# The second feed-forward sweep of a hybrid decoder layer: low parts on VectorE, sums of the last weights in other sweeps

## The chip, the cores and the metric

The kernel runs on one core of a Trainium2 chip. The metric is the device time of one execution in microseconds; the median of three executions is given, and one further execution was profiled. Engines are named as in the profile: PE (TensorE, matmuls), DVE (VectorE), ACT (ScalarE), POOL or Pool (GpSimd), SP (SyncE, which here only issues transfers).

## What is computed

One layer: a modulated norm, a projection into gated DeltaNet heads and sliding-window attention heads, an output projection with a gated residual, then a second modulated norm and a gated feed-forward part with its residual. The change lies in the feed-forward part; before it come the last products of the output projection, whose tiles the text names `w_o`. With 1024 tokens, 1024 features and an inner width of 2816:

```python
mixed = jnp.concatenate([o_g, o_s], axis=-1) @ w_out[l]
x = x + gate1 * mixed

h2 = rms_norm(x, norm2_w[l]) * (1.0 + scale2) + shift2
ffn = (jax.nn.silu(h2 @ w_gate[l]) * (h2 @ w_up[l])) @ w_down[l]
x = x + gate2 * ffn
```

## The kernel before

All products are made to nearly full precision from a high and a low part of each operand: `split` (lines 192 and 193) rounds an operand on ACT to its high part and subtracts that from the operand on DVE or Pool for the low part. `mm_block` (lines 1360 to 1364) runs three matmuls for each pair of tiles: high by high, high by low, low by high. So the low part of the weights is wanted first by the third matmul.

The feed-forward products are made by a scheme of seven products of half-sized blocks in place of eight, which needs sums and differences of blocks. There are three stages.

- **First sweep**, eleven steps p = 0 to 10, one for each 256 columns of the inner width. `weights1` loads and splits two sets of tiles (w0, w1; high on ACT, low on Pool); 48 matmuls write the banks `ps_c`. ACT copies a first result out (`X`, line 1402, stored to XD), and the product of line 1408 makes `av`, stored to AD. In the first steps the rest of the second norm and the splits of its results (B, T) run on DVE, ACT and Pool, too.
- **Second sweep**, again p = 0 to 10. `weights2` loads, for each of the two matrices j (gate and up), `wa` and `wb` with two blocks each, makes four sums of 128x512 on DVE (lines 1429 to 1432), and splits five left sides (S2, S3, S1, A22, S4) for each j, high on ACT, low on Pool. Ten units of twelve matmuls write the banks `ps_S`; after each one DVE adds the bank to an earlier result (line 1466). A22 goes on in the bank of S3, S4 in that of S1. The results are made into six tiles of `ops`, stored to AD (line 1479); `ops` and `sg` have one buffer. The tiles of `weights2` come from a pool `px`, the split ones from `wg2`, with ten buffers of 128x1024.
- **Last products** P1, P2, P6, P7, P4, P5, P3: 924 matmuls into `ps_P`. Their left sides are blocks of the weights `wdown`, or sums of them that `down_sums` has stored in SD before (used from P6 on); their right sides are the slices of AD. `left` loads and splits the former (Pool makes the low parts), `slices` the latter (DVE does).

`down_sums` is a piece of work that belongs to no stage: 24 times it loads four blocks of `wdown` (tile `sd`, 512 KB, half of that in the last of each six), makes four sums on DVE and stores them. Fifteen calls stand in the first sweep's code and nine in the second's.

The order of PE's instructions is that of the code. For the other engines and for SP's queue a scheduler decides it within the limits that the code sets with `issue_after` and `high_priority`; each engine then works strictly in that order, and so does SP: a transfer whose buffer isn't free holds up all that stand behind it.

## Time and profile before

| | us |
|---|---|
| median of three executions | 1318.24 (1317.91 to 1318.87) |
| profiled execution, its own time | 1316.84 |
| span of the profiled execution | 1315.1 |
| first sweep, in the trace | about 654 to 779 |
| second sweep | 779.4 to 1099.6 |
| last products | from 1099.6 on |
| PE busy, whole span | 1193.2 |
| DVE busy, whole span | 904.9 |
| Pool busy, whole span | 626.5 |
| ACT busy, whole span | 537.3 |

The page gives busy time for each engine; matmuls are pipelined, so the distance from one start to the next tells the rate, not the length of one. A view of stretches gives busy time, the clock that TensorE was granted (1.00 is 2.4 GHz, 0.50 is 1.2 GHz) and the transfer rate. A view of waits adds up the idle time of an engine by what ended it. A timeline lists instructions in order, with the idle time ahead of each. Buffer numbers are left out of names in the trace: `wS` stands for wS20, wS31 and so on.

### The profile page before, as it was taken

How to read it: one execution, taken by the hardware profiler on the slowest of the kernel's cores; microseconds unless marked ns; L12 is line 12 of the kernel's file. 1: busy time of each engine (PE TensorE's matmuls, PEld its weight loads, DVE VectorE, ACT ScalarE, POOL GpSimd, SP SyncE). 2: the span in 40 equal slices, each digit the busy share in tenths (PEclk: the TensorE clock that was granted, in tenths of full speed). 3: DMA queues.
4: the chain of work that ended last, by engine and by line, in shares of the span. 5: the costliest groups of instructions: out<-in, count | busy, mean ns of one | idle time of the engine just before them, and what ended most of it. 6: DMA issues, size and time to landing. Idle time of an engine off the chain costs nothing.

```text
span 1315.1 us, 18978 instructions
## 1 busy us (share of the span) xinstructions
PE 1193.2 (91%) x6710; PEld 975.4 (74%) x6710; DVE 904.9 (69%) x1690; ACT 537.3 (41%) x1028; POOL 626.5 (48%) x453
## 2 busy tenths in 40 slices
PE   6868697896899799998889999999999999999998
PEld 5757576685788577777678888777777778888887
DVE  7999889979724667586864656777767786656430
ACT  4373555422433767533435542222322233544430
POOL 4667354534335334345435556454454454455440
PEclk7898899898999889999899999999999999999999
DMA  8637458485639845448685645555555467876651
GB/s 324 227 93 262 154 121 233 127 226 197 197 109 211 145 82 131 157 159 289 233 275 205 207 136 169 176 192 192 192 202 189 178 230 266 264 267 198 201 168 40
DMA packets 167214, 250.62 MB, mean 191 GB/s; under 512 B 40656, under 2 KB 106448, under 8 KB 165584
## 3 DMA queue, kind: packets, MB, share of 16 engines
q1 hardware_dynamic: 157520, 241.03, 56.5%
q0 software_dynamic: 9600, 8.39, 3.9%
q8 instruction: 53, 0.87, 0.3%
q14 instruction: 41, 0.34, 0.1%
HBM read 182.89 MB, written 66.45 MB: 190 GB/s over the span
## 4 chain that ended last, share of the span: by engine, by line
PE 39%; DVE 18%; DMA 11%; issue 4%; POOL 3%; ACT 2%; SPq 0%; DVEq 0%; ACTq 0%; POOLq 0%
PE ps_P L1363 5%; PE ps_P L1362 5%; PE ps_P L1364 5%; DMA wb<-in_wgate_dram 3%; DMA SD<-sd 3%; DMA sd<-in_wdown_dram 2%; PE ps_c L1362 2%; PE ps_c L1364 2%; PE ps_c L1363 2%; POOL wS L193 2%; DMA qb<-QS 2%; DVE wa L1432 1%; DVE xu L1466 1%; PE ps_gz L212 1%; DVE soltmp L817 1%
## 5 line engine op out<-in xcount | busy, mean ns | idle before, releaser
L193 POOL TENSOR_TENSOR wP<-rP,wP 128x512 fp32r<-128x512 f32 (+1 forms) x84 | 109.1, 1314 | 104.6 <-ACT wP L192 95.9
L1363 PE MATMUL ps_P<-t,wP 128*128 128x512 f32 x308 | 120.4, 391 | 0.0
L1362 PE MATMUL ps_P<-t,wP 128*128 128x512 f32 x308 | 120.4, 391 | 0.0
L1364 PE MATMUL ps_P<-t,wP 128*128 128x512 f32 x308 | 120.2, 390 | 0.0
L193 POOL TENSOR_TENSOR wS<-wa,wS 128x512 fp32r<-128x512 f32 x44 | 62.2, 1422 | 118.4 <-ACT wS L192 59.4
L1364 PE MATMUL ps_S<-T,wS 128*128 128x512 f32 x264 | 102.9, 390 | 0.3 <-POOL wS L193 0.3
L1363 PE MATMUL ps_S<-T,wS 128*128 128x512 f32 x264 | 102.9, 390 | 0.0
L1362 PE MATMUL ps_S<-T,wS 128*128 128x512 f32 x264 | 102.8, 389 | 0.0
L1429 DVE TENSOR_TENSOR ws<-wb 128x512 f32<-128x512 f32 x22 | 24.6, 1118 | 72.8 <-DMA wb<-in_wgate_dram 68.0
L192 ACT ACTIVATE wP<-rP 128x512 fp32r<-128x512 f32 (+1 forms) x84 | 47.3, 587 | 66.8 <-PE ps_P L1364 41.2
L1470 ACT ACTIVATE sg<-sg 128x512 f32<-128x512 f32 x33 | 20.9, 632 | 131.3 <-DVE sg L1466 131.2
L1362 PE MATMUL ps_c<-B,w 128*128 128x512 f32 x176 | 68.8, 391 | 1.3 <-ACT X L1402 1.3
L1364 PE MATMUL ps_c<-B,w 128*128 128x512 f32 x176 | 68.5, 389 | 0.0
L1363 PE MATMUL ps_c<-B,w 128*128 128x512 f32 x176 | 68.5, 389 | 0.0
L1362 PEld LDWEIGHTS ps_P<-t,wP 128*128 128x128 f32 x308 | 57.9, 188 | 12.6
L1364 PEld LDWEIGHTS ps_P<-t,wP 128*128 128x128 f32 x308 | 57.9, 188 | 12.5
L1363 PEld LDWEIGHTS ps_P<-t,wP 128*128 128x128 f32 x308 | 57.8, 188 | 12.4
L192 ACT ACTIVATE wS<-wa 128x512 fp32r<-128x512 f32 x44 | 26.6, 625 | 93.9 <-DVE wa L1431 68.3
L1364 PEld LDWEIGHTS ps_S<-T,wS 128*128 128x128 f32 x264 | 49.6, 188 | 11.1 <-POOL wS L193 0.7
L1362 PEld LDWEIGHTS ps_S<-T,wS 128*128 128x128 f32 x264 | 49.6, 188 | 10.5
L1363 PEld LDWEIGHTS ps_S<-T,wS 128*128 128x128 f32 x264 | 49.6, 188 | 10.4
L212 PE MATMUL ps_o<-mix,w_o 128*128 128x512 f32 x128 | 52.9, 413 | 4.1 <-ACT w_o L192 4.1
(507 smaller groups left out, 3575.5 us busy)
## 6 DMA issues: line engine op xcount, KB each, us to landing
ada<-in_ada_dram SPq DMA_DIRECT2D x48, 512.0 KB, 4.6
AD<-ops SPq DMA_DIRECT2D x11, 1536.0 KB, 5.2
rP<-SD SPq DMA_DIRECT2D x16, 704.0 KB, 5.4
sd<-in_wdown_dram SPq DMA_DIRECT2D x20, 512.0 KB, 5.7
SD<-sd SPq DMA_DIRECT2D x20, 512.0 KB, 3.5
rP<-in_wdown_dram SPq DMA_DIRECT2D x12, 704.0 KB, 5.9
XD<-X SPq DMA_DIRECT2D x22, 256.0 KB, 3.8
xu<-XD SPq DMA_DIRECT2D x22, 256.0 KB, 4.2
```

Of the source, the lines that this page charges most:

```text
L192: act.activation(out=r(hi), in_=src, func=AF.Copy)
L193: last = eng.tensor_tensor(out=r(lo), in0=src, in1=hi, op=ALU.subtract)
L212: pe.matmul(out, lhsT=r(lhs[0]), rhs=r(rhs[0]), start=first, stop=False)
L817: dve.tensor_tensor(out=tv[g], in0=bc(L[:, i, i + 1:32].unsqueeze(1), (P, i, 31 - i)), in1=bc(L[:, 0:i, i:i + 1], (P, i, 31 - i)), op=ALU. ...
L1362: pe.matmul(ps, lhsT=r(wh), rhs=r(xh), start=first and i == 0, stop=False, **kw)
L1363: pe.matmul(ps, lhsT=r(wh), rhs=r(xl), start=False, stop=False, **kw)
L1364: pe.matmul(ps, lhsT=r(wl), rhs=r(xh), start=False, stop=i == n - 1, **kw)
L1429: dve.tensor_tensor(out=s1, in0=a21, in1=a22, op=ALU.add)
L1432: dve.tensor_tensor(out=a12, in0=a12, in1=a11, op=ALU.subtract)
L1466: done["U"] = dve.tensor_tensor(out=out, in0=ps, in1=other, op=ALU.add)
L1470: act.activation(out=out, in_=out, func=AF.Silu)
```

## The change

`weights2` makes one tile for both matrices where there were two: five tiles of 128x1024 (a11, a12, a21, a22 and a sum) for each p, loaded by eight transfers of 256 KB in place of four of 512 KB. So there are four sums of 128x1024 instead of eight of 128x512, and five high parts on ACT and five low parts of 128x1024, these now on DVE instead of ten of 128x512 on Pool. The units run in the order S2, S3, S1, A22, S4, each for j = 0 and then j = 1. The additions that empty the banks get high priority.

`down_sums` takes two marks: its load is issued after one of them, its first sum after the other. In the first sweep it stands behind the store of X and behind av, with a list that tells how many calls belong to each p (again fifteen). In the second sweep there is one call in every other p, five in all; the last four follow the first four products of P1 in the code, with tiles of another pool.

```diff
@@ -24,7 +24,7 @@
 HD = 64
 NB = T // P
 FF = 2816
-FF_CHUNKS = (6, 6, 6, 4)
+SUMS1 = (1, 2, 1, 1, 1, 1, 1, 1, 2, 2, 2)
 ADA_TAGS = "bcd" * 5 + "bcde" * 4 + "d"
 ADA_ITER = 14
 ADA_DVE = ()
...
@@ -1375,13 +1376,17 @@
             split(w[:, 0, js], w[:, 1, js], raw[:, js], pool)
         return w
 
-    def down_sums(d, k0, k1):
-
-        t = rpre.tile([P, NP, P], F32, tag="r", name=f"sd{d}_{k0}")[:, 0:8].rearrange("p (a k) n -> p a k n", a=4)
+    def down_sums(d, k0, k1, load_after, sums_after, t=None):
+
+        if t is None:
+            t = rpre.tile([P, NP, P], F32, tag="r", name=f"sd{d}_{k0}")[:, 0:8]
+        t = t.rearrange("p (a k) n -> p a k n", a=4)
         n = k1 - k0
-        sp.dma_start(out=t[:, :, 0:n], in_=wdown[d][:, :, k0:k1])
+        with tc.issue_after(load_after.ins):
+            sp.dma_start(out=t[:, :, 0:n], in_=wdown[d][:, :, k0:k1])
         a11, a12, a21, a22 = (t[:, i, 0:n] for i in range(4))
-        dve.tensor_tensor(out=a22, in0=a21, in1=a22, op=ALU.add)
+        with tc.issue_after(sums_after.ins):
+            dve.tensor_tensor(out=a22, in0=a21, in1=a22, op=ALU.add)
         dve.tensor_tensor(out=a21, in0=a11, in1=a21, op=ALU.subtract)
         dve.tensor_tensor(out=a11, in0=a22, in1=a11, op=ALU.subtract)
         dve.tensor_tensor(out=a12, in0=a12, in1=a11, op=ALU.subtract)
@@ -1399,19 +1404,18 @@
                 mm_block(ps[j], lambda i: (w[a][:, 0, 4 * j + i], w[a][:, 1, 4 * j + i]), lambda i: B1[4 * a + i], 4, a == 0)
                 if a == 0:
                     x = t2(f"X{j}_{p}")
-                    done["X"] = act.activation(out=x, in_=ps[j], func=AF.Copy)
-                    sp.dma_start(out=XD[p, j], in_=x)
+                    act.activation(out=x, in_=ps[j], func=AF.Copy)
+                    done["X"] = sp.dma_start(out=XD[p, j], in_=x)
                 if (p, a, j) in ((0, 0, 1), (1, 0, 1)):
                     next(n2, None)
         av = t2(f"av{p}")
         act.activation(out=av, in_=ps[0], func=AF.Silu)
-        dve.tensor_tensor(out=av, in0=ps[1], in1=av, op=ALU.mult)
+        done["av"] = dve.tensor_tensor(out=av, in0=ps[1], in1=av, op=ALU.mult)
         sp.dma_start(out=AD[:, p, 0], in_=av)
-        with tc.issue_after(done["X"].ins):
-            for _ in range(2 if p in (0, 1, 2, 10) else 1):
-                down_sums(*sums.pop(0))
-            if 2 <= p < 10:
-                next(second)
+        if 2 <= p < 10:
+            next(second)
+        for _ in range(SUMS1[p]):
+            down_sums(*sums.pop(0), done["X"], done["av"])
 
 
     close_pools(2)
@@ -1420,25 +1424,24 @@
 
     def weights2(p):
 
-        src, out = {}, {}
-        for j in range(2):
-            wa, wb, ws = (px.tile([P, 2, 4, P], F32, tag="s4", name=f"w{x}{j}_{p}") for x in "abs")
-            sp.dma_start(out=wa.rearrange("p a k n -> p (a k) n"), in_=SRC[j][2 * p])
-            sp.dma_start(out=wb.rearrange("p a k n -> p (a k) n"), in_=SRC[j][2 * p + 1])
-            a11, a12, a21, a22, s1 = wa[:, 0], wa[:, 1], wb[:, 0], wb[:, 1], ws[:, 0]
-            dve.tensor_tensor(out=s1, in0=a21, in1=a22, op=ALU.add)
-            dve.tensor_tensor(out=a21, in0=a11, in1=a21, op=ALU.subtract)
-            dve.tensor_tensor(out=a11, in0=s1, in1=a11, op=ALU.subtract)
-            dve.tensor_tensor(out=a12, in0=a12, in1=a11, op=ALU.subtract)
-            src[j] = {"S2": a11, "S3": a21, "S1": s1, "A22": a22, "S4": a12}
-        for j, n in ORDER:
-            w = wg2.tile([P, 2, 4, P], F32, tag="w", name=f"w{n}{j}_{p}")
-            split(w[:, 0], w[:, 1], src[j][n], pool)
-            out[j, n] = w[:, 0], w[:, 1]
+        a11, a12, a21, a22, s1 = (px.tile([P, 2, 4, P], F32, tag="s4", name=f"w{x}_{p}") for x in ("11", "12", "21", "22", "s"))
+        for t, i, a in ((a21, 1, 0), (a22, 1, 1), (a11, 0, 0), (a12, 0, 1)):
+            for j in range(2):
+                sp.dma_start(out=t[:, j], in_=SRC[j][2 * p + i][:, 4 * a:4 * a + 4])
+        dve.tensor_tensor(out=s1, in0=a21, in1=a22, op=ALU.add)
+        dve.tensor_tensor(out=a21, in0=a11, in1=a21, op=ALU.subtract)
+        dve.tensor_tensor(out=a11, in0=s1, in1=a11, op=ALU.subtract)
+        dve.tensor_tensor(out=a12, in0=a12, in1=a11, op=ALU.subtract)
+        out = {}
+        for n, src in (("S2", a11), ("S3", a21), ("S1", s1), ("A22", a22), ("S4", a12)):
+            hi, lo = (wg2.tile([P, 2, 4, P], F32, tag="w", name=f"w{n}{x}_{p}") for x in "hl")
+            split(hi, lo, src, dve)
+            for j in range(2):
+                out[j, n] = hi[:, j], lo[:, j]
         return out
 
     RIGHT = {"S2": "T2", "S3": "T3", "S1": "T1", "A22": "T4", "S4": "B22"}
-    ORDER = [(j, n) for pair in (("S2", "S3"), ("S1",), ("A22",), ("S4",)) for j in range(2) for n in pair]
+    ORDER = [(j, n) for n in ("S2", "S3", "S1", "A22", "S4") for j in range(2)]
     w = weights2(0)
     for p in range(NP):
         ops = ev.tile([P, 6, TH], F32, tag="ops", name=f"ops{p}")
@@ -1449,11 +1452,10 @@
         xu, bk = {}, {}
         for j in range(2):
             xu[j] = t4(f"xu{j}_{p}", (P, 2, TH), tag="e")
-            sp.dma_start(out=xu[j][:, 0], in_=XD[p, j])
+            done["T"] = sp.dma_start(out=xu[j][:, 0], in_=XD[p, j])
         for j, n in ORDER:
-            if (j, n) == (0, "S1") and sums:
-                with tc.issue_after(done["U"].ins):
-                    down_sums(*sums.pop(0))
+            if (j, n) == (0, "S4") and p % 2 and len(sums) > 4:
+                down_sums(*sums.pop(0), done["T"], done["U"])
             u2, u3 = xu[j][:, 0], xu[j][:, 1]
             c22, c21, c12 = outs[j]
             first = n not in ("A22", "S4")
@@ -1463,7 +1465,8 @@
             ps = bk[j, key]
             mm_block(ps, lambda i: (w[j, n][0][:, i], w[j, n][1][:, i]), lambda i: T_[RIGHT[n], i], 4, first)
             out, other = {"S2": (u2, u2), "S3": (u3, u2), "S1": (c22, u3), "A22": (c21, u2), "S4": (c12, u2)}[n]
-            done["U"] = dve.tensor_tensor(out=out, in0=ps, in1=other, op=ALU.add)
+            with tc.high_priority():
+                done["U"] = dve.tensor_tensor(out=out, in0=ps, in1=other, op=ALU.add)
             if n in ("S1", "A22", "S4"):
                 i = ("S1", "A22", "S4").index(n)
                 if j == 0:
...
@@ -1562,7 +1565,14 @@
 
     for i in (0, 1):
         load_x1(i, 0)
-    last("P1", 0, lambda d: wdown[d][:, 0], 1, True, lambda d, ps: act.activation(out=U[d], in_=ps, func=AF.Copy))
+    def after_p1(d, ps):
+        act.activation(out=U[d], in_=ps, func=AF.Copy)
+        if sums:
+            s_ = sums.pop(0)
+            down_sums(*s_, done["left"], done["lo"], t4(f"sd{s_[0]}_{s_[1]}", (P, 8, P)))
+
+    last("P1", 0, lambda d: wdown[d][:, 0], 1, True, after_p1)
+    assert not sums
 
     def after_p2(d, ps):
         add_x(d, 0, ps)
```

What the diff doesn't tell is where the scheduler puts the sums. The first place is the end of the output projection on DVE. `x1` is the residual stream (line 1211, 1212 in the new kernel), `ssum2` the sum of squares for the norm, `ms`, `rsq` and `rs` its way to the factor of each row. Before:

```order
L1218 TENSOR_TENSOR ssum2_0_4897<-ssum2_0_4897,sqx07_5644 128x512
L1386 TENSOR_TENSOR sd0_6_6208<-sd0_6_6208 128x256
L1387 TENSOR_TENSOR sd0_6_6208<-sd0_6_6208 128x256
L1211 SCALAR_TENSOR_TENSOR x1_10_5685<-ps_o10_5660,modc_115,x1_10_5685 128x512
L1384 TENSOR_TENSOR sd0_8_6291<-sd0_8_6291 128x256
L277 TENSOR_SCALAR ms_n20_5704<-ssps20_5699 128x4
L1385 TENSOR_TENSOR sd0_8_6291<-sd0_8_6291 128x256
L180 TENSOR_SCALAR rsq_n20_5707<-ms_n20_5704 128x4
L182 TENSOR_SCALAR rsq_n20_5707<-ms_n20_5704 128x4
L1386 TENSOR_TENSOR sd0_8_6291<-sd0_8_6291 128x256
L184 TENSOR_TENSOR rsq_n20_5707<-rsq_n20_5707 128x4
L1387 TENSOR_TENSOR sd0_8_6291<-sd0_8_6291 128x256
```

After:

```order
L1219 TENSOR_TENSOR ssum2_0_4897<-ssum2_0_4897,sqx06_5609 128x512
L1212 SCALAR_TENSOR_TENSOR x1_06_5606<-ps_o07_5617,modc_115,x1_06_5606 128x512
L1219 TENSOR_TENSOR ssum2_0_4897<-ssum2_0_4897,sqx07_5644 128x512
L1212 SCALAR_TENSOR_TENSOR x1_10_5685<-ps_o10_5660,modc_115,x1_10_5685 128x512
L278 TENSOR_SCALAR ms_n20_5704<-ssps20_5699 128x4
L180 TENSOR_SCALAR rsq_n20_5707<-ms_n20_5704 128x4
L182 TENSOR_SCALAR rsq_n20_5707<-ms_n20_5704 128x4
L184 TENSOR_TENSOR rsq_n20_5707<-rsq_n20_5707 128x4
L185 TENSOR_TENSOR rsq_n20_5707<-rsq_n20_5707 128x4
```

All `sd` rows are gone from there; the first of them now stands behind av of the first sweep's step 0.

The second place is the boundary between the sweeps, also on DVE; `wS2l_0` is the low part of S2 for p = 0. After:

```order
L1434 TENSOR_TENSOR w12_0_7069<-w12_0_7069,w11_0_7068 128x1024
L1413 TENSOR_TENSOR av10_7042<-ps_c1_10_7002,av10_7042 128x512
L193 TENSOR_TENSOR wS2l_0_7086<-w11_0_7068,wS2h_0_7085 128x1024
L1389 TENSOR_TENSOR sd2_2_7046<-sd2_2_7046 128x256
L193 TENSOR_TENSOR wS3l_0_7090<-w21_0_7070,wS3h_0_7089 128x1024
L1390 TENSOR_TENSOR sd2_2_7046<-sd2_2_7046 128x256
L1389 TENSOR_TENSOR sd2_4_7053<-sd2_4_7053 128x256
L193 TENSOR_TENSOR wS1l_0_7094<-ws_0_7072,wS1h_0_7093 128x1024
```

Before:

```order
L1431 TENSOR_TENSOR wa1_0_7077<-ws1_0_7079,wa1_0_7077 128x512
L1432 TENSOR_TENSOR wa1_0_7077<-wa1_0_7077 128x512
L1408 TENSOR_TENSOR av10_7042<-ps_c1_10_7002,av10_7042 128x512
L1466 TENSOR_TENSOR xu0_0_7119<-ps_S20_0_7123,xu0_0_7119 128x512
L1466 TENSOR_TENSOR xu0_0_7119<-ps_S30_0_7137,xu0_0_7119 128x512
L1466 TENSOR_TENSOR xu1_0_7121<-ps_S21_0_7151,xu1_0_7121 128x512
L1429 TENSOR_TENSOR ws0_1_7281<-wb0_1_7280 128x512
L1430 TENSOR_TENSOR wb0_1_7280<-wa0_1_7279,wb0_1_7280 128x512
```

Behind av10 there stand now low parts, which were Pool's, and sums of the last weights in turn, ahead of the first addition from a bank.

The third place is a step in the middle of the second sweep on DVE. `ps_S` are the banks, `sg` and `xu` what is added to them or made of them. Before:

```order
L1466 TENSOR_TENSOR sg5_8173<-ps_S30_5_8192,xu0_5_8174 128x512
L1429 TENSOR_TENSOR ws0_7_8547<-wb0_7_8546 128x512
L1466 TENSOR_TENSOR ops5_8171<-ps_S31_5_8220,xu1_5_8176 128x512
L1430 TENSOR_TENSOR wb0_7_8546<-wa0_7_8545,wb0_7_8546 128x512
L1472 TENSOR_TENSOR ops5_8171<-ops5_8171,sg5_8173 128x512
L1431 TENSOR_TENSOR wa0_7_8545<-ws0_7_8547,wa0_7_8545 128x512
L1466 TENSOR_TENSOR sg5_8173<-ps_S10_5_8241,xu0_5_8174 128x512
L1432 TENSOR_TENSOR wa0_7_8545<-wa0_7_8545 128x512
L1466 TENSOR_TENSOR b12d_5_8172<-ps_S11_5_8256,xu1_5_8176 128x512
L1472 TENSOR_TENSOR b12d_5_8172<-b12d_5_8172,sg5_8173 128x512
L1475 TENSOR_TENSOR ops5_8171<-ops5_8171,b12d_5_8172 128x512
L1429 TENSOR_TENSOR ws1_7_8556<-wb1_7_8555 128x512
```

After:

```order
L193 TENSOR_TENSOR wS1l_9_8859<-ws_9_8837,wS1h_9_8858 128x1024
L1469 TENSOR_TENSOR ops8_8677<-ps_S11_8_8755,xu1_8_8682 128x512
L1469 TENSOR_TENSOR sg8_8679<-ps_S30_8_8712,xu0_8_8680 128x512
L1475 TENSOR_TENSOR ops8_8677<-ops8_8677,sg8_8679 128x512
L1469 TENSOR_TENSOR ops8_8677<-ps_S31_8_8726,xu1_8_8682 128x512
L1475 TENSOR_TENSOR ops8_8677<-ops8_8677,sg8_8679 128x512
L193 TENSOR_TENSOR wA22l_9_8863<-w22_9_8836,wA22h_9_8862 128x1024
L1469 TENSOR_TENSOR sg8_8679<-ps_S10_8_8740,xu0_8_8680 128x512
L1431 TENSOR_TENSOR ws_10_9037<-w21_10_9035,w22_10_9036 128x1024
L1432 TENSOR_TENSOR w21_10_9035<-w11_10_9033,w21_10_9035 128x1024
L1469 TENSOR_TENSOR b12d_8_8678<-ps_S11_8_8755,xu1_8_8682 128x512
```

The sums of the weights (lines 1429 to 1432, now 1431 to 1434) are half as many and twice as wide, and low parts of line 193 stand among the additions.

## Rows read from the trace of the kernel before

**Rows 1.** Busy time in stretches (start:end, length, then the columns named); counts are starts.

```profile
core 0: us, PE busy (x) PEld busy (x) DVE busy (x) ACT busy (x) POOL busy (x), PEclk, DMA share, GB/s
628.40:633.70 5.30, 5.30 (x13) 4.19 (x14) 5.27 (x12) 4.16 (x7) 1.46 (x1) 0.50 0.24 81
665.00:676.00 11.00, 11.00 (x52) 8.88 (x51) 6.93 (x21) 4.19 (x7) 3.39 (x4) 1.00 0.92 299
700.00:779.40 79.40, 79.40 (x352) 65.74 (x352) 45.96 (x48) 41.87 (x75) 40.81 (x29) 1.00 0.55 186
779.40:1099.60 320.20, 307.41 (x1321) 245.99 (x1320) 239.89 (x312) 91.32 (x163) 165.13 (x119) 1.00 0.54 192
1099.60:1315.00 215.40, 211.24 (x925) 173.35 (x923) 95.48 (x109) 79.01 (x144) 97.77 (x76) 1.00 0.59 194
```

**Rows 2.** Waits of PE, 600 to 700 us: total us, times, longest.

```profile
PE ps_o L212 <- ACT w_o L192: 4.1, 1, 4.1
PE ps_o L214 <- POOL w_o L193: 3.1, 2, 1.8
PE ssps L1229 <- DVE ssum L1218: 2.1, 1, 2.1
PE rowps_n L286 <- DVE rs_n L186: 1.4, 1, 1.4
PE ps_c L1362 <- ACT X L1402: 1.3, 1, 1.3
```

**Rows 3.** Timeline of DVE: start us, us, operation [idle before <-releaser].

```profile
608.93 0.42 DVE L1384 TENSOR_TENSOR sd<-sd 128x256 f32<-128x256 f32 x1 [4.81 <-DMA sd<-in_wdown_dram]
...
613.54 1.70 DVE L1384 TENSOR_TENSOR sd<-sd 128x128 f32<-128x128 f32 x1 [1.34 <-DMA sd<-in_wdown_dram]
```

**Rows 4.** Timelines of PE, ACT and POOL around w_o14.

```profile
625.89 0.50 PE L212 MATMUL ps_o<-mix,w_o 128*128 128x512 f32 x1 [4.07 <-ACT w_o L192]
...
624.80 1.04 ACT L192 ACTIVATE w_o<-w_o14r 128x1024 fp32r<-128x1024 f32 x1
...
625.97 2.37 POOL L193 TENSOR_TENSOR w_o<-w_o14r,w_o 128x1024 fp32r<-128x1024 f32 x1 [1.40 <-ACT w_o L192]
```

**Rows 5.** Timeline of DVE over one step p of the second sweep.

```profile
929.37 0.69 DVE L1429 TENSOR_TENSOR ws<-wb 128x512 f32<-128x512 f32 x1 [6.47 <-DMA wb<-in_wgate_dram]
929.98 0.68 DVE L1466 TENSOR_TENSOR ops<-ps_S,xu 128x512 f32<-128x512 f32 x1
...
934.37 1.81 DVE L1472 TENSOR_TENSOR b12d<-b12d,sg 128x512 f32<-128x512 f32 x1
...
958.62 0.69 DVE L1429 TENSOR_TENSOR ws<-wb 128x512 f32<-128x512 f32 x1 [6.44 <-DMA wb<-in_wgate_dram]
```

**Rows 6.** Waits of PE in the second sweep, 779 to 1100 us.

```profile
PE ps_S L1362 <- DVE xu L1466: 9.0, 12, 1.8
PE ps_S L1362 <- DVE sg L1466: 3.1, 6, 1.8
PE ps_S L1364 <- POOL wS L193: 0.3, 1, 0.3
```

**Rows 7.** DVE by line and shape: busy us, mean ns, idle before.

```profile
L253 DVE CUSTOM_DVE_ANT_0 ada<-ada,cb 128x1024 f32<-128x1024 f32 x15 | 18.2, 1214 | 0.0
...
L742 DVE TENSOR_TENSOR ee<-ee,cmask 128x1024 f32<-128x1024 f32 x4 | 10.4, 2610 | 1.3 <-POOL ee L740 1.3
...
L765 DVE TENSOR_TENSOR kq<-kn,nbrow 128x1024 f32<-128x1024 f32 x4 | 5.5, 1381 | 0.1
```

**Rows 8.** DMA issues: times, KB each, median us to landing.

```profile
AD<-ops SPq DMA_DIRECT2D x11, 1536.0 KB, 5.2
...
sd<-in_wdown_dram SPq DMA_DIRECT2D x20, 512.0 KB, 5.7
...
xu<-XD SPq DMA_DIRECT2D x22, 256.0 KB, 4.2
```

**Rows 9.** SP's issues at the beginning of P2.

```profile
1128.32 0.33 SPq L1527 DMA_DIRECT2D rP<-in_wdown_dram  x1
```

More of the change, by code (lines that the diff above doesn't have):

```diff
@@ L195, in split @@
             done["pool"] = last
+        return last
     def wunit(src, name, kt=KT, eng=None, parts=None, raw=None, steps=1):
@@ L1497, in slices @@
         for i in range(m):
-            split(t[:, i, 0], t[:, i, 1], raw[:, i], dve)
+            done["lo"] = split(t[:, i, 0], t[:, i, 1], raw[:, i], dve)
             out.append((t[:, i, 0], t[:, i, 1]))
@@ L1526, in left @@
         raw = rpre.tile([P, NP, P], F32, tag="r", name=f"r{name}")
-        sp.dma_start(out=raw, in_=src)
+        done["left"] = sp.dma_start(out=raw, in_=src)
         out = []
```

## The prediction

> **What bounds the kernel now.** I read the views in this order: busy time by stage, what TensorE (PE) waited for in the stages that the change touches, then the engine that let it wait. From 700 us to the end of the first sweep PE is busy all the time: 352 matmuls start in 79.40 us, 0.2256 us each [rows 1], so PE is the floor and every other engine counts only where PE waits for it. In the second sweep it isn't full: 1321 matmuls take 320.2 us [rows 1]. Two places give time away.
>
> The first is the tail of the output projection and the first steps of the first sweep (608 to 690 us), where PE waits five times, 12.0 us in all [rows 2]. The vector engine (DVE) works in order, and the sums of the last weights (`sd`) stand between its other rows. At 608.93 and 613.54 us it had been idle 4.81 and 1.34 us for an `sd` load; the row sums of the norm and the products of line 1238 come behind them [rows 3]. The high parts of w_o14 on ScalarE (ACT) come at 624.80, after those products, Pool's low parts at 625.97, and PE waits 4.07 us [rows 4]. After that pause the granted clock is 0.50 from 628.4 to 633.7 us: 13 matmuls in 5.30 us [rows 1], where 13 at 0.2256 would take 2.9. So this hole has a second price of 2.4 us.
>
> The second place is the second sweep. One step p comes back every 29.25 us (line 1429 at 929.37 and 958.62), each time after 6.4 us in which DVE waits for a `wb` load [rows 5]. Evacuations of PSUM stand behind that waiting row in DVE's order, and PE waits for them: 9.0 us for `xu`, 3.1 for `sg` [rows 6]. It is a ring: a buffer comes free when Pool has made its low part, then come the load, the sums on DVE, the high part on ACT, and Pool again. 120 matmuls at 0.2256 take 27.1 us; at the rate of the last products, 925 in 211.24 us busy or 0.2284 [rows 1], 27.4.
>
> **Part 1: no `sd` in the output projection.** The sums leave 577 to 690 us and stand behind av of each p. Of the 12.0 us of waits, rs_n (1.4), ssum (2.1) and X (1.3) are DVE rows, or follow such rows, that stood behind `sd` rows; the w_o wait of 4.1 is the delayed line 1238. Of Pool's 3.1, the later 1.3 belongs to w_o17, whose load stood behind `sd` loads on SP's queue. All of that gone, with the clock's 2.4, is 14.4. What is late next: row_n still has to pass line 1238, and DVE and Pool work on it side by side; with all of it some 5 us earlier w_o14's high part is just ready when PE comes, and Pool's low part, one operation of 2.37 us [rows 4], is not. I leave 1.7 us there, so the upper end is -12.7. The lower end is -7: only the 4.1 with its clock and half a microsecond. I take -12, near the upper end, because each wait has an `sd` row or load right ahead of it.
>
> **Part 2: those sums in the first sweep.** Fifteen sums, as many as before, but now over its 125 us instead of up to 690 us. Each loads 0.52 MB and stores as much [rows 8]. The sweep moved 186 GB/s once the sums were past [rows 1]; fifteen times 1.05 MB in 125 us are 126 more, less the two half-sized sums and what runs over into the next sweep: about 290 on average, and about 340 in the four steps with two sums. The nearest row is 665 to 676 us: 299 GB/s, DMA 92% busy, with PE busy all of the 11.00 us [rows 1]. So the average can be carried; the peaks cannot, and lag. Weight loads are issued more than 10 us ahead of their use, and behind an `sd` load on DVE stands only the next av, 11 us later. Between 0 and +8; I take +1.5, since the row shows PE unhurt at that rate.
>
> **Part 3: the step from sweep to sweep.** The first low part of the second sweep now stands on DVE behind the last av, which needs PE's last product; ACT's high part and DVE's low part follow, 1.04 [rows 4] and about 1.2 us, while PE needs the low part with its third matmul. Then a sum whose load waits for an earlier store stands ahead of the next low part. Before, PE lost 0.3 us there [rows 6]. Bounds 1 to 6; I take +2.7: 1.4 for the first low part, the rest for the sum.
>
> **Part 4: the second sweep.** Removed: Pool's 110 splits, the wait for them, and with them the slow DVE rows (a 128x512 addition beside a Pool operation takes 1.81 us, alone 0.69, one per 0.60) [rows 5]. Added on DVE: five low parts. Its work per p: ten evacuations, three products, four subtractions, 17 x 0.60 = 10.2; one split for the last products, 0.7; sums of the last weights in every other p, 4 x 0.42 [rows 3], on average 0.8; four sums and five low parts of 128x1024. No subtraction of that shape without Pool is in this trace; the nearest rows are 1.21 (line 253) and 1.38 (line 765) [rows 7]. At 1.21 that is 10.9, in all 22.6 of PE's 27.1 us; at 1.38, 24.1. So PE becomes the bound. In the new order a p's weights are made during the p before, and between an evacuation and the next use of its bank lie 8 us, so DVE may run late by some microseconds. One more ring must close: `ops` has one buffer, and its next first row needs the store of the last one landed. The store is issued about 10 us into a step, lands 5.2 later [rows 8], and is wanted at 16.3: about 1 us in hand. `xu` loads (4.2) [rows 8] land with as little in hand; a delay there costs DVE, not PE. The stage ends between 1320 x 0.2256 = 298 and 1320 x 0.2284 = 301.5 us, plus small stops; I take 303, a gain of 17 of the 320.2.
>
> Loads shrink from 512 to 256 KB. The Trainium skill, "DMA: Bandwidth & Descriptors", section "Bandwidth", wants at least 1 MiB in a transfer and shows 138 GB/s at 64 KB and 341 at 1 MB; by that the change goes the wrong way. The trace does not bear out that it matters here: the 299 GB/s above were reached with weight loads of 256 KB among them.
>
> **Part 5: the end.** Four sums fall into p = 10, and on SP slices of AD for P2 now stand behind weight loads that wait for Pool's splits. Before, the load of the last left weights went out at 1128.32 [rows 9], just when P2 began, so little is in hand. 0 to +4; I take +1.
>
> Sum: -12 + 1.5 + 2.7 - 17 + 1 = -23.8. The profiled execution took 1316.84, so 1293.0; it lies 1.4 below the median of 1318.24, so the median comes to **1294.4**.
>
> **The rivals.** A: *the moved sums bind.* If the four steps with two sums are DMA bound, 340 instead of 299 GB/s gives 14% of 46 us, 6.4, and late sums hold low parts at the transition for 4.5 more: with the 1.5 already in the sum, 9.4 above the forecast, 1304. For it: nothing above 300 GB/s is in the trace. Against: slack of 10 us. B: *the second sweep keeps its pace*, since the `ops` store or a load is late in every p; then the 17 are gone: 1311. For it: 1 us in hand. Against: 7 us of slack in the banks. C: *the pauses of the output projection come back* from the next thing late (row_n, Pool, w_o loads), clock included: of 12 only 3 remain, 1303. D: *DVE becomes the bound, slower than before.* The place is every p of the second sweep, the price the nine 128x1024 rows. All else gained is -6.8, so it is slower by 0.2% when the sweep takes over 329.6 us, 29.97 per p; 29.97 - 11.7 leaves 18.3 for nine rows, so from 2.03 us each. Line 742 has 2.61 [rows 7], beside Pool: then 35.2 per p, 387 us, and 1378. At 2.2 us it would be 1336. Against: Pool has next to nothing to do then. E: *the small loads bind*, by the skill's rule above: eight loads of 256 KB one after the other at 4.2 us [rows 8] are 33.6 us per p, so 370 us in the sweep and 1361. Against: the loads overlap in the trace.
>
> **How the numbers follow.** Forecast 0.57, A 0.15, B 0.09, C 0.08, D 0.08, E 0.03. Faster by over 0.2% (2.6 us, about what a measurement can tell): the forecast, A, C and 0.04 of B, 0.84; within: 0.05 of B, where part 1 falls to its lower end; slower: D and E, 0.11. The range leaves out D and E and the outer part of others: low 1284 (12.7 of part 1 gone, the sweep at 299, no new cost, which is -34), high 1311 (B).
>
> **What would show it.** Right: no wait of PE for w_o's high part or rs_n, no granted clock of 0.5 near 630 us; steps of the second sweep every 27.1 to 27.5 us with DVE busy some 23 of them; no Pool row there; at the start of the sweep one PE wait of 1 to 2 us for a low part on DVE and one for the next. Wrong: DVE rows of 128x1024 above 1.5 us; waits of DVE for AD<-ops in every p; DMA above 90% busy with PE waiting for w0 or w1 in the first sweep.

## The result and the profile after

The changed kernel takes 1301.71 us (median of four, 1297.64 to 1307.84), the kernel before 1318.08 beside it: a ratio of 0.9896 with a 95% interval from 0.9864 to 0.9928, so faster by about 1%. The forecast was 1294.4 in a range of 1284 to 1311; the sign and the range hold, the gain is some 14 us by the ratio and 16 by the medians, where 24 was forecast. The profiled execution took 1303.1, its span is 1301.3.

From the starts of the first products in the two traces the stages come out so (us; "forecast" is the change that the prediction's terms give for the stage; the second profile of the changed kernel is from the last experiments):

| stage | before | after | after, second profile | measured change | forecast |
|---|---|---|---|---|---|
| up to the first product of the first sweep | 654.2 | 642.9 | 641.0 | -11.3 | -8.6 |
| first sweep, to the second's first product | 125.2 | 135.4 | 137.4 | +10.2 | about -1 |
| second sweep, to the first of P1 | 320.2 | 305.8 | 304.8 | -14.4 | -15 |
| last products, to the start of the last matmul | 210.9 | 212.6 | 212.8 | +1.7 | +1 |

(Of part 1, ssum and X, 3.4 us together, lie in the first sweep; of part 3 I count 0.7 there and 2 in the second. A wait ahead of the second sweep's first product counts into the first sweep.) Three of four stages came about as forecast; the first sweep became 11 us longer than I had said. The waits of PE name the place; these answer [rows 2] and [rows 6], a row is the total, the number and the longest:

```profile
PE ps_c L1363 <- ACT X L1407: 8.1, 4, 4.4
PE ps_o L215 <- POOL w_o L193: 2.6, 2, 2.1
PE ps_S L1363 <- ACT wS2h L192: 2.1, 1, 2.1
PE ps_S L1365 <- DVE wS2l L193: 1.1, 1, 1.1
PE ps_P L1364 <- DVE t L193: 0.9, 1, 0.9
PE ps_o L213 <- ACT w_o L192: 0.3, 1, 0.3
```

The waits for w_o's high part, rs_n, ssum and the banks of the second sweep are gone or nearly so. Pool's w_o stays with 2.6. New are 8.1 us for X on ACT in the first sweep, and 2.1 and 1.1 at the start of the second. By stretches (as [rows 1]: length, busy time and count by engine, granted clock, DMA share, GB/s):

```profile
core 0: us, PE busy (x) PEld busy (x) DVE busy (x) ACT busy (x) POOL busy (x), PEclk, DMA share, GB/s
711.00:734.00 23.00, 18.57 (x72) 14.84 (x71) 9.96 (x15) 8.22 (x16) 10.09 (x8) 0.85 0.92 310
778.20:786.00 7.80, 6.64 (x16) 4.95 (x17) 4.16 (x8) 3.78 (x4) 0.00 (x0) 0.57 0.87 271
786.00:1084.10 298.10, 298.10 (x1307) 245.00 (x1306) 243.12 (x316) 83.84 (x103) 10.85 (x8) 1.00 0.58 197
1084.10:1301.00 216.90, 212.02 (x925) 173.05 (x923) 97.61 (x119) 80.20 (x145) 98.45 (x76) 1.00 0.62 209
```

The third stretch is the second sweep from its eighth microsecond on: PE is busy in all 298.1 us, 1307 matmuls, 0.2281 us each, with Pool at 11 us (its work for P1). The first stretch is the loss: 72 matmuls in 23 us, where 0.2256 each would be 16.2, with a granted clock of 0.85 on average and 310 GB/s; the second is the start of the second sweep, where two stops are followed by products at a clock of 0.57 on average. DVE's rows in the second sweep, as [rows 7] (busy us, mean ns, idle before):

```profile
L1469 DVE TENSOR_TENSOR ops<-ps_S,xu 128x512 f32<-128x512 f32 x22 | 15.2, 690 | 30.6 <-PE ps_S L1365 20.6 <-DMA AD<-ops 10.0
...
L193 DVE TENSOR_TENSOR wS3l<-w,wS3h 128x1024 fp32r<-128x1024 f32 x11 | 13.4, 1221 | 1.3 <-ACT wS3h L192 1.3
...
L1431 DVE TENSOR_TENSOR ws<-w,w 128x1024 f32<-128x1024 f32 x10 | 12.2, 1215 | 0.0
```

A low part of 128x1024 takes 1.22 us, a sum 1.215: the lower of my two prices. DVE was idle 10.0 us for the store of `ops`, but PE didn't notice.

### The profile page after: what moved, and what is told of

The parts are those of the page before. It is cut to its first block, busy times and chain, and to the rows that moved or that the text cites. A ratio compares the mean times of both kernels' runs of the same rounds, so it can differ in the third digit from the quotient of the medians.

```text
span 1301.3 us, 18727 instructions
## 1 busy us (share of the span) xinstructions
PE 1193.2 (92%) x6710; PEld 979.4 (75%) x6710; DVE 911.2 (70%) x1701; ACT 534.7 (41%) x973; POOL 477.2 (37%) x343
## 4 chain that ended last, share of the span: by engine, by line
PE 62%; DVE 6%; ACT 4%; DMA 3%; issue 2%; POOL 1%; SPq 0%; ACTq 0%; DVEq 0%; POOLq 0%
PE ps_S L1365 8%; PE ps_S L1364 8%; PE ps_S L1363 8%; PE ps_P L1364 5%; PE ps_P L1365 5%; PE ps_P L1363 5%; PE ps_c L1363 2%; PE ps_o L213 2%; PE ps_c L1364 2%; PE ps_c L1365 2%; PE ps_o L215 2%; PE ps_o L214 2%; PE ps_gz L213 1%; DVE soltmp L818 1%; PE ps_gz L215 1%
## 5 line engine op out<-in xcount | busy, mean ns | idle before, releaser
L1363 PE MATMUL ps_c<-B,w 128*128 128x512 f32 x176 | 70.3, 399 | 8.1 <-ACT X L1407 8.1
L1364 PE MATMUL ps_c<-B,w 128*128 128x512 f32 x176 | 69.5, 395 | 0.0
L1365 PE MATMUL ps_c<-B,w 128*128 128x512 f32 x176 | 69.4, 394 | 0.0
L257 POOL TENSOR_TENSOR ada<-ada,cb 128x1024 f32<-128x1024 f32 x17 | 43.8, 2592 | 29.3 <-DMA ada<-in_ada_dram 18.7
L215 PE MATMUL ps_o<-mix,w_o 128*128 128x512 f32 x128 | 50.9, 398 | 2.6 <-POOL w_o L193 2.6
L213 PE MATMUL ps_o<-mix,w_o 128*128 128x512 f32 x128 | 52.4, 409 | 0.3 <-ACT w_o L192 0.3
L1550 DVE SCALAR_TENSOR_TENSOR x1r<-ps_P,modc,x1r 128x512 f32<-128x512 f32 x16 | 11.9, 747 | 56.3 <-PE ps_P L1365 56.3
L214 PE MATMUL ps_o<-mix,w_o 128*128 128x512 f32 x128 | 50.5, 394 | 0.0
L1363 PEld LDWEIGHTS ps_c<-B,w 128*128 128x128 f32 x176 | 33.7, 191 | 17.3 <-ACT X L1407 10.3
L1365 PEld LDWEIGHTS ps_c<-B,w 128*128 128x128 f32 x176 | 33.6, 191 | 7.2
L1364 PEld LDWEIGHTS ps_c<-B,w 128*128 128x128 f32 x176 | 33.6, 191 | 6.7
L1363 PE MATMUL ps_S<-T,wS2h 128*128 128x512 f32 x88 | 35.6, 405 | 2.1 <-ACT wS2h L192 2.1
L1469 DVE TENSOR_TENSOR ops<-ps_S,xu 128x512 f32<-128x512 f32 x22 | 15.2, 690 | 30.6 <-PE ps_S L1365 20.6
```

The costliest lines, as they stand in the source:

```text
L213: pe.matmul(out, lhsT=r(lhs[0]), rhs=r(rhs[0]), start=first, stop=False)
L214: pe.matmul(out, lhsT=r(lhs[0]), rhs=r(rhs[1]), start=False, stop=False)
L215: pe.matmul(out, lhsT=r(lhs[1]), rhs=r(rhs[0]), start=False, stop=last)
L257: eng.tensor_tensor(out=w, in0=w, in1=cb, op=ALU.mult)
L1363: pe.matmul(ps, lhsT=r(wh), rhs=r(xh), start=first and i == 0, stop=False, **kw)
L1364: pe.matmul(ps, lhsT=r(wh), rhs=r(xl), start=False, stop=False, **kw)
```

## The experiments

The time of one execution scatters: over all its executions the kernel before took 1311.34 to 1324.95 us, the changed kernel 1297.64 to 1308.09. A part of that lies ahead of everything changed here: the same place in the output projection (first use of the norm's sums) comes at 594.4 to 603.5 us in nine profiles, of eight kernels, whose orders on every engine are alike up to there. So I compare stages, each from its own first product, and for the whole use the ratios, each to the kernel before as it ran beside that run.

| run | ratio to before (95%) | first sweep | second sweep | last products |
|---|---|---|---|---|
| before | 1 | 125.2 | 320.2 | 210.9 |
| after | 0.9896 (0.9864 to 0.9928) | 135.4 | 305.8 | 212.6 |
| after, second time | 0.9904 (0.9874 to 0.9934) | 137.4 | 304.8 | 212.8 |
| sums only | 0.9959 (0.9928 to 0.9990) | 134.9 | 313.7 | 215.9 |
| weights only | 0.9831 (0.9790 to 0.9872) | 124.2 | 303.3 | 210.9 |
| stores behind X | 0.9831 (0.9793 to 0.9870) | 129.6 | 306.4 | 212.6 |
| nine sums in the first sweep | 0.9802 (0.9772 to 0.9832) | 122.6 | 303.3 | 218.5 |
| Pool's low parts | 1.0031 (1.0005 to 1.0057) | 137.5 | 318.7 | 213.8 |
| no sums in p = 10 | 0.9786 (0.9753 to 0.9819) | 122.6 | 304.1 | 210.9 |
| old order | 0.9933 (0.9910 to 0.9956) | 137.3 | 305.0 | 214.4 |
| before, sums at S4 | 0.9893 (0.9860 to 0.9927) | 127.0 | 308.1 | 210.9 |
| old weights, new sums | 0.9822 (0.9794 to 0.9850) | 123.6 | 309.5 | 210.9 |

**How the loss in the first sweep hangs together, in the trace of the changed kernel.** Read SP, then DVE, then ACT (start, us, operation, idle before):

```profile
704.06 0.60 SPq L1386 DMA_DIRECT2D sd<-in_wdown_dram  x1
...
710.67 0.53 SPq L1393 DMA_DIRECT2D SD<-sd  x1
...
711.92 0.44 SPq L1408 DMA_DIRECT2D XD<-X  x1
```

```profile
709.38 0.29 DVE L1389 TENSOR_TENSOR sd<-sd 128x128 f32<-128x128 f32 x1 [6.37 <-DMA sd<-in_wdown_dram]
...
715.41 0.69 DVE L1269 TENSOR_TENSOR b<-x,x 128x512 f32<-128x512 f32 x1 [4.76 <-DMA XD<-X]
...
720.02 1.75 DVE L1272 TENSOR_TENSOR x<-x,x 128x512 f32<-128x512 f32 x1
```

```profile
721.80 0.63 ACT L192 ACTIVATE T<-x 128x512 fp32r<-128x512 f32 x1 [2.75 <-DVE x L1272]
722.34 1.06 ACT L1407 ACTIVATE X<-ps_c 128x512 f32<-128x512 f32 x2
```

SP issued an `sd` load at 704.06. DVE waited 6.37 us for it. Three more issues followed on SP, then came the store of that sum, which could go only at 710.67, and behind it, with one load between them, the first store of X, at 711.92; ACT had made that X by 707.3. `b3` (the block difference from which the second sweep's right sides T are made, line 1269) takes the buffer from which that store reads; DVE waited 4.76 us for it. T's chain ended late, one of its rows stood beside Pool (1.75), ACT waited 2.75 for it, and the copy of X stood behind T on ACT: 722.34. PE had started its last product at 718.16 and went on at 722.97. That is my theory, *queue*. Its rival, *rate* (rival A of the prediction), says that too much was transferred.

**Sums only.** Edit: in the changed kernel, `weights2`, the order of units and the priority are put back.

```diff
-            split(hi, lo, src, dve)
+            split(w[:, 0], w[:, 1], src[j][n], pool)
```

> Only the sums of the last weights are moved; the second sweep's weights are made as before (Pool's low parts, two tiles, old order, no priority). If the two halves of the change are independent: the output projection ends some 11 us earlier (first product of the first sweep at about 643), the first sweep shows the same waits for ACT's X as in the changed kernel (8 us and a spell at half the clock) and takes 131 to 133 us, since the low part at its end is Pool's again; the second sweep stays at 318 to 321 us. Sum: 1312 to 1316. Rival: the waits for X come from the first loads of the joint tiles (eight transfers on SP during the first sweep) and not from the sums; then the first sweep is back at 123 to 125 us and the time is 1305 to 1308.

Measured: 1313.33 us (1308.23 to 1318.03). The output projection gains, the first sweep takes 134.9 us with these waits for X (8.1 in the changed kernel):

```profile
PE ps_c L1363 <- ACT X L1407: 9.4, 5, 4.7
```

So the loss belongs to the moved sums, not to the joint tiles' loads. The second sweep is 313.7, shorter than I expected; its stops lie before 864 us, though Pool still makes all low parts. That asked for three of the experiments below (Pool's low parts; before, sums at S4; old weights, new sums).

**Weights only.** Edit: the kernel before with the new `weights2`, order and priority; the sums as before.

> Only the second sweep's weights are changed (joint tiles, low parts on DVE, new order, priority of the bank additions); the sums of the last weights stand where they stood before. If the halves are independent: the output projection and the first sweep as before (first product at about 654, 125 us), the second sweep 301 to 304 us from first to first product although nine sums stand in it, one stop of 1 to 3 us at its start: 1300 to 1304. Rival: with the sums beside them DVE is too full in the second sweep and PE waits for banks again; then 308 us or more and 1306 or more.

Measured: 1300.88 us, second sweep 303.3 with nine sums in it. So half of the change gives at least as much as the whole (a ratio of 0.9831 against 0.9896): the rival (DVE too full) falls, and the moved sums gained nothing on top of it, since what they won ahead of the first sweep was lost in it and more. From the norm's sums on, the stages come to 689.6 us here and to 697.9 in the changed kernel; the whole time hides that, because this profile reached the norm's sums at 607.4, the latest of all.

**Stores behind X.** Edit, in the first sweep alone: up to p = 9 a sum's store is put on a list, and `store_sums` issues it in the next step, behind the stores of X (cut to the lines that matter):

```diff
-        sp.dma_start(out=SD[d][:, :, k0:k1], in_=t[:, :, 0:n])
+        stores.append((SD[d][:, :, k0:k1], t[:, :, 0:n]))
...
+        store_sums()
         av = t2(f"av{p}")
```

> The changed kernel, with one difference: in the first sweep the store of a sum is issued behind the next step's two stores of X, and not ahead of them. Theory queue: the waits for ACT's X come from SP's order. A store of a sum waits on SP for DVE's sum, which waits for its load; the stores of X stand behind it; b3 on DVE waits for the buffer that they read, T on ACT waits for b3's chain, X on ACT stands behind T. Then DVE's wait of 12 us for XD<-X goes, PE's 8.1 us for X shrink to under 3 and the half clock near 723 us with it: the first sweep about 128 us to the first product of the second, time 1294 to 1297. Theory rate: the transfers are simply too many (282 to 335 GB/s from 711 to 734 us); then the same number of microseconds is lost, at other places, and the time stays at 1300 to 1304.

Measured: 1300.67 us (1293.60 to 1302.45), first sweep 129.6. PE's waits:

```profile
PE ps_S L1363 <- ACT wS2h L192: 3.4, 1, 3.4
PE ps_c L1363 <- ACT X L1417: 3.1, 5, 1.0
...
PE ps_S L1365 <- DVE wS2l L193: 1.7, 1, 1.7
```

DVE's wait of `b3` for a store of X, in the changed kernel and here, and the first sweep here as a stretch (columns as above):

```profile
DVE b L1269 <- DMA XD<-X: 12.1, 3, 4.8
...
DVE b L1269 <- DMA XD<-X: 0.2, 1, 0.2
```

```profile
645.70:775.29 129.59, 123.14 (x541) 99.74 (x539) 79.12 (x123) 61.56 (x108) 61.53 (x42) 1.00 0.82 267
```

That wait went from 12.1 us to 0.2, PE's for X from 8.1 to 3.1, and no product of the first sweep ran at the lower clock. The transfers are the same in number, and they moved at 267 GB/s on average where the changed kernel's first sweep had 257. That is the queue theory in kind; 3.1 us of waits stayed where I had said under 3, and 129.6 us where I had said 128. But the time is no better than the rate theory said: the last sums now stand even longer ahead of the first sums and low parts of the second sweep, and PE waits 3.4 and 1.7 us there (the 3.4 still counts into the first sweep), with thirteen products at half the clock behind it. The whole time alone would have misled; the mechanism is shown by the waits.

**Nine sums in the first sweep.** Edit, beside the last one:

```diff
-SUMS1 = (1, 2, 1, 1, 1, 1, 1, 1, 2, 2, 2)
+SUMS1 = (1,) * 9 + (0, 0)
...
-            if (j, n) == (0, "S4") and p % 2 and len(sums) > 4:
+            if (j, n) == (0, "S4") and len(sums) > 4:
```

> As the run before (stores of sums behind the stores of X), and fewer sums in the first sweep: one in each of the steps 0 to 8, none in 9 and 10, one in every step of the second sweep (eleven), four as before behind P1. By the queue theory the first sweep loses no more than 2 us, and the start of the second loses its two stops (3.2 us of waiting, and the half clock behind them, 2.7 us) but for about 1 us, since no sum stands ahead of the first weights any more: first sweep 124 to 126 us, second 301 to 303, time 1288 to 1291. Rival: six more sums in the second sweep (1.4 us of DVE each) fill DVE there and PE waits for banks: second sweep 306 us or more, and no gain over the run before.

Measured: 1295.25 us. The first sweep falls to 122.6 us, below the kernel before, and one stop of 1.4 us is left, at the start of the second; six more sums in the second sweep cost nothing (303.3). The miss is at the end, 218.5 us for the last products:

```profile
1079.57 0.65 SPq L1541 DMA_DIRECT2D rP<-in_wdown_dram  x1
1086.94 0.52 SPq L1396 DMA_DIRECT2D SD<-sd  x1
...
1088.18 0.47 SPq L1541 DMA_DIRECT2D rP<-in_wdown_dram  x1
...
1100.32 0.32 SPq L1509 DMA_DIRECT2D t_7r<-AD  x1
```

```profile
PE ps_P L1364 <- DVE t L193: 3.0, 4, 1.2
PE ps_P L1363 <- ACT t L192: 1.4, 1, 1.4
```

SP (start, us, operation) issued nothing from 1080.2 to 1086.94: it stood for the store of the very last sum, whose load DVE waited for. The loads of left weights and of slices for P2 queue behind it; `t_7r` goes at 1100.32, when P2 has begun (in the kernel before at 1120.45 with P2 from about 1130 on). It is the same queue again. The changed kernel, with the same four sums behind P1 but none in p = 10, has 212.6: most of the loss belongs to the sum in p = 10.

**No sums in p = 10.** Edit: fifteen in the second sweep, two in each even step and one in each odd one up to 9, none behind P1.

```diff
-            if (j, n) == (0, "S4") and len(sums) > 4:
-                down_sums(*sums.pop(0), done["T"], done["U"])
+            if (j, n) == (0, "S4"):
+                for _ in range((2, 1)[p % 2] if p < 10 else 0):
+                    down_sums(*sums.pop(0), done["T"], done["U"])
```

> The run with nine sums in the first sweep, but without sums at the end: fifteen in the second sweep, two in each of the steps 0, 2, 4, 6, 8, one in each of 1, 3, 5, 7, 9, none in 10 and none behind P1. Theory: the 218.5 us of the last products there (211 before) come from SP, which stood 6.7 us for the sum of the last store in p = 10 while loads for P1 and P2 queued behind it; then the last products take 211 to 213 us and the second sweep stays at 302 to 305, time 1287 to 1291. Rival: the loads for P2 are late because the end of the second sweep comes earlier for DVE's and ACT's splits, whatever the sums do; then 216 us or more at the end and no gain. Second rival: two sums in a step fill DVE, the second sweep takes 307 us or more.

Measured: 1287.17 us (1282.33 to 1290.38), the best of all: its slowest execution is faster than the fastest of the changed kernel (1297.64, the second time 1300.90). The last products are back at 210.9, the second sweep holds at 304.1 with two sums in a step. What PE still waits for:

```profile
PE ps_o L215 <- POOL w_o L193: 2.4, 2, 2.1
PE ps_S L1365 <- DVE wS2l L193: 1.4, 1, 1.4
PE ps_c L1363 <- ACT X L1417: 0.9, 2, 0.6
PE ps_o L213 <- ACT w_o L192: 0.3, 1, 0.3
```

**Pool's low parts.** Edit in the changed kernel: `split(hi, lo, src, pool)`.

> The changed kernel, but the five low parts of each p are made by Pool again (128x1024, on joint tiles). The run with the sums alone had Pool's low parts and no stop of PE after 863 us in the second sweep, so Pool may not have been what held PE. Theory sums: the stops of before came from the nine sums on DVE in the second sweep; then Pool's low parts (5 x 2.4 us of 27.3) cost no more than 3 us: second sweep 303 to 309 us and 1300 to 1305. Theory Pool: low parts on Pool bring the ring and the slow DVE rows back, PE waits for banks in every p: second sweep 316 us or more, time over 1311.

Measured: 1319.24 us, second sweep 318.7; the theory *Pool* holds for joint tiles, though PE waited for a bank six times and not in every p. DVE's sums (busy us, mean ns, idle before) and PE's waits in that sweep:

```profile
L1433 DVE TENSOR_TENSOR w<-ws,w 128x1024 f32<-128x1024 f32 x10 | 18.6, 1856 | 0.0
...
L1431 DVE TENSOR_TENSOR ws<-w,w 128x1024 f32<-128x1024 f32 x10 | 16.5, 1653 | 12.6 <-POOL wA22l L193 12.6
```

```profile
PE ps_S L1363 <- DVE xu L1469: 8.9, 6, 2.8
```

Three of the four sums take 1.65 to 1.86 us here in place of 1.22 (the fourth 1.21), and 12.6 us more go by ahead of the first sum, in which DVE waits for Pool's low part of A22. So a low part on Pool does cost with joint tiles, by DVE's slower rows and by the ring.

**Old order.** Edit in the changed kernel: the old `ORDER`, no priority for the additions from the banks.

> The changed kernel with the units in the old order (S2 and S3 of j = 0, then of j = 1) and without the priority for the additions that empty the banks. If these two belong to the gain, PE waits for banks or for low parts of S3 and the second sweep takes 308 us or more. If not, it stays at 303 to 307 us and the time at 1299 to 1304, which is what I expect, since no bank was waited for in the changed kernel.

Measured: second sweep 305.0, as expected: these two edits bring nothing that shows there. The whole came to 1308.89 us (ten executions), 6 more than the changed kernel; its profile has the place in the output projection at 603.5, the latest of the nine, but I can't say that this is the edit's doing or chance. That is left open.

**Before, sums at S4.** Edit in the kernel before, one word:

```diff
-            if (j, n) == (0, "S1") and sums:
+            if (j, n) == (0, "S4") and sums:
```

> The kernel before with one difference: its nine sums in the second sweep are put ahead of S4 in place of S1. Theory place: it is the four rows of a sum between S3's and S1's bank additions that held up the loop there, so moving them two units on lets PE run nearly full from the third step on: second sweep 308 to 314 us, time 1306 to 1312. Theory load: a sum costs DVE time wherever it stands in the step while Pool makes the low parts, so the second sweep stays at 317 to 321 us and the time at 1316 to 1320.

Measured: 1301.65 us, second sweep 308.1: the theory *place*. Waits of DVE, and of PE for a bank, in the second sweep of this run, and DVE's first row in the kernel before:

```profile
DVE ops L1466 <- DMA AD<-ops: 30.2, 9, 4.3
DVE ws L1429 <- DMA wb<-in_wgate_dram: 15.6, 9, 3.6
```

```profile
PE ps_S L1362 <- DVE xu L1466: 4.2, 6, 1.5
```

```profile
DVE ws L1429 <- DMA wb<-in_wgate_dram: 63.8, 10, 8.1
```

DVE's wait for the `wb` load falls from 63.8 to 15.6 us. What it waits for now is mostly the store of `ops`, 30.2 us, which reached PE only through 4.2 us of waits for `xu` (9.0 and 3.1 before). With Pool's low parts, the old tiles and all nine sums, that one word is worth 12 of the 17 us that the new weights alone gained in this sweep, and its ratio to before, 0.9893, is that of the whole change. One step of the kernel before shows how the sum held the loop (DVE, then ACT, POOL and SP; buffer names as above, L1470 is ACT's Silu):

```profile
946.79 1.36 DVE L1384 TENSOR_TENSOR sd<-sd 128x256 f32<-128x256 f32 x1
...
949.45 0.68 DVE L1466 TENSOR_TENSOR sg<-ps_S,xu 128x512 f32<-128x512 f32 x1
```

```profile
950.22 0.63 ACT L1470 ACTIVATE sg<-sg 128x512 f32<-128x512 f32 x1 [5.80 <-DVE sg L1466]
950.76 0.62 ACT L192 ACTIVATE wS<-ws 128x512 fp32r<-128x512 f32 x1
...
951.46 1.30 POOL L193 TENSOR_TENSOR wS<-ws,wS 128x512 fp32r<-128x512 f32 x1 [3.58 <-ACT wS L192]
```

```profile
949.56 0.57 SPq L1388 DMA_DIRECT2D SD<-sd  x1
...
953.14 0.56 SPq L1382 DMA_DIRECT2D sd<-in_wdown_dram  x1
953.79 0.57 SPq L1427 DMA_DIRECT2D wb<-in_wgate_dram  x1
```

The sum's four rows (946.79 to 949.53) stand ahead of the addition for sg; ACT's Silu waits for that, S1's high part stands behind the Silu, Pool's low part behind that, to 952.76, and the `wb` load comes then, for which DVE waits 6.44 us until 958.62 [rows 5]. With the sums at S4 that load goes as the same low part ends, at 942.88. The edit also moves the sum's store and the next sum's load on SP, which stand ahead of `wb` here, too; from 952.76 to 953.79 that is about 1 us. What the rows on DVE and the places on SP are worth each by itself was not run.

**Old weights, new sums.** Edit: the best run with `weights2`, order and priority as before.

> The best run so far (nine sums in the first sweep with late stores, fifteen in the second, none in its last step), but the second sweep's weights made as before: two tiles per matrix, Pool's low parts, old order, no priority. It tells what the joint tiles and DVE's low parts are worth once the sums stand well. Theory: with the sums ahead of S4, Pool's low parts cost what the run with only that edit showed, 308 us in the second sweep against 304; two sums in a step cost some more: 306 to 312 us, time 1289 to 1296. Rival: the fifteen sums fill DVE, which is slowed by Pool's work beside it, and the second sweep goes back to 316 to 322 us: time above 1298.

Measured: 1293.81 us, second sweep 309.5 (304.1 with the new weights). So the joint tiles with low parts on DVE are worth 5 us in the second sweep once the sums stand well, not 17. And these 5 us are one place: PE's waits for a bank in that sweep, and the sweep from 830 us on as a stretch (columns as above):

```profile
PE ps_S L1363 <- DVE xu L1481: 4.0, 2, 3.5
```

```profile
830.00:1077.04 247.04, 247.04 (x1084) 203.01 (x1083) 202.70 (x282) 74.79 (x130) 128.25 (x91) 1.00 0.68 234
```

One stop of 3.5 us at 819 with thirteen products at half the clock behind it makes the difference; from 830 us on PE is busy all the time, at 0.228 us a product, with two tiles for each matrix and Pool's low parts.

**The changed kernel once more.** No edit.

> The changed kernel once more, in five rounds on this chip, to have its stages a second time beside the others: first sweep 134 to 137 us from its first product to that of the second sweep, second sweep 304 to 307, last products 212 to 214, time 1299 to 1305. If the waits for ACT's X in the first sweep were chance, the first sweep would come out below 130.

Measured: 1302.87 us, first sweep 137.4: the waits for X weren't chance; they came at the same four places with other lengths (the two longest 2.8 and 3.5 us, where they had been 1.3 and 4.4).

## Why the prediction was right or wrong

**Part 1, right in kind, a little too small.** The output projection lost its waits; from the first use of the norm's sums to the first product of the first sweep it took 51.2 us before, 44.1 after, and 44.1 again in the best run. That is -7.1 against -8.6; the rest of the 11.3, 4.2 us, lies ahead of that place, where `sd` rows stood, too, but where profiles scatter by nine. I had left 1.7 us for Pool's low part: it is 2.07, and the clock still falls behind it for a few products.

**Part 2, the step that failed.** It is the sentence "behind an `sd` load on DVE stands only the next av, 11 us later". It isn't so. In every other step T's chain stands there, too, its first row (`b3`) waits for a store of X, and on SP that store stood behind the store of a sum. I had followed SP's order for the weights' loads, which have slack, but not for the stores, and not who waits for their buffers. The sweep became 10.2 and 12.2 us longer; 2.1 and 4.1 of that are the stop at its end, which belongs to part 3, so part 2's price is about +8 in both profiles in place of -2 (3.4 saved, 1.5 spent). With the 3.4 saved the term itself is some 11.5, outside its bounds of 0 to +8. The rate theory, which I had made a rival at 1304, gives the time almost exactly, and for the wrong reason: with the same transfers in another order on SP the waits for X shrink to 3.1. Its sign came by half only: from 711 to 734 us the DMA share was 0.92, but PE waited for X and not for w0 or w1.

**Part 3, mis-sized.** Forecast +2.7; two stops of 2.1 and 1.1 us, where 0.3 stood before. The stops alone are +2.9, and the products behind them ran at half the clock, twelve at 0.43 us in place of 0.23, 2.4 us that I had not counted. Nor were they the stops I had named: the longer one was for S2's high part on ACT, the other for S2's low part, and none came for the next low part. Sums of the last weights on DVE ahead of the first weights' sums and between them were the cause: without them (the runs with nine in the first sweep) one stop of 1.4 for S2's low part is left, the very term I had for it, and no lower clock.

**Part 4, right in time, wrong in cause.** 303 was forecast, 305.8 measured with 2.4 of lower clock and a stop of 1.1 in it: from 786 us on PE never waits. The sizes were right (1.22 us for a row of 128x1024, DVE busy 243 of 298 us, 10 us for the `ops` store hidden). But I had put the whole gain down to Pool and the ring. The one-word edit shows that 12 of the 17 were the place of a sum in the step: its four rows on DVE stood ahead of a bank addition for which ACT, and behind ACT Pool and the load, waited; what its store and load on SP added is open. I took the 6.4 us of waiting for a load as the ring's own doing; with the sum two units later most of that wait is gone, and in the run with the old weights PE doesn't wait at all from 830 us on. That the size came right in spite of it is luck in part: 303 is little more than the rate of PE itself, and the other edits that ended the waits came out there as well (303.3 to 304.1).

**Part 5, right in size** (+1.7 for +1). Kernels with no sum in p = 10 or behind P1 have 210.9, so the 1.7 belongs to the moved sums; PE's one wait there is 0.9 us for a slice's low part. That SP's order can cost there the run with nine sums shows, with 7.6 us, but by a sum's store for which SP stood, not by loads that wait for Pool's splits, as I had it. Why the run with the sums alone has 215.9 is open.

**The sum.** The range held by its width: part 2 lay outside its own bounds, part 3 was worse by some 2.6, and 4 us of what the first stage gained may be scatter.

**The rivals.** B, D and E did not come: no wait for banks, no slow rows, and in the second sweep no row of DVE waited for one of the loads of 256 KB. (In D, 1336 goes by the profiled time; by the median it is 1338.) On the rule of the Trainium skill, "DMA: Bandwidth & Descriptors", section "Bandwidth", to put at least 1 MiB into a transfer (measured there for transfers that GpSimd issues; here SP issues them): 310 GB/s in the stretch of 711 to 734 us were reached with weight loads of 256 KB and sums of 512 KB, several under way at once, so the smaller loads did not bind here. C had its remainder in the 2.6 us for Pool's w_o.

## What to carry to other kernels

Of a step that is moved, follow its store through the queue as well as its load: an in-order queue makes each waiting store a wait of all that stands behind it, and the next question is whose buffer that holds. Before an engine is blamed for a ring, move the small work that stands in the ring: one word gave here 12 of 17 us. And compare stages, not whole times, when the part ahead of the change scatters by a good part of what the change gains.

## What the runs showed of the hardware that I had not expected

- The granted clock. A stop of PE of 2.07 us in the output projection was followed by products at 0.43 us each, half of full rate, for 2.1 us (619.8 to 621.9, granted clock 0.50), one of 4.43 us by ten of them. So a stop can cost twice: 2.1 and 1.1 us at the start of the second sweep brought another 2.4. The length of a stop alone doesn't tell whether it will: single stops of 1.1 to 1.78 us were not followed by such products, but neither was one of 2.13 us in the kernel before (at 661.9, granted clock 1.00 behind it) nor one of 2.81 in the run with Pool's low parts (at 831.5, 1.00), while one of 1.84 in that run was (at 1003.0, eight products).
- A subtraction of 128x1024 on DVE takes 1.215 to 1.22 us with no Pool operation beside it and, in three of a step's four sums, 1.65 to 1.86 on average with Pool's low parts in the same step.
- Up to the point where they part, programs with the same order reached the same place 594.4 to 603.5 us after their start. The granted clock goes with it: from 300 to 590 us it was 0.96 on average in the earliest of the nine profiles and 0.92 in the latest. What makes this scatter was not tried.
